# Seven block products instead of eight in the feed-forward up projection of a two-layer decoder

## The chip, the cores and the metric

The program runs on one core of a Trainium2 chip. The metric is the device time of one execution in microseconds (us); 2150.83 us is the median of three runs before the change (2150.53 to 2151.25). Engines are named as in the profile: PE is TensorE (PEld its weight loads), DVE is VectorE, ACT is ScalarE, POOL is GpSimd, SP is the SyncE queue, which issues all DMAs here. A matmul has a stationary operand of 128x128, which is loaded first, and streams a moving operand of up to 512 columns past it; its output goes to PSUM, which has eight banks of 128x512 float32.

## The reference

Two decoder layers on 512 tokens of 1024 channels. A layer mixes tokens in three branches and then runs a gated feed-forward block; only the latter changes:

```python
def conv_ffn(h, w_up, conv_w, conv_b, w_down):
    a, b = jnp.split(h @ w_up, 2, axis=-1)          # w_up: 1024 x (2 * 2816)
    ap = jnp.pad(a, ((0, 0), (CONV_WIDTH - 1, 0), (0, 0)))
    a = conv_b + sum(conv_w[j] * ap[:, j:j + s_len] for j in range(CONV_WIDTH))
    return (jax.nn.silu(a) * b) @ w_down            # w_down: 2816 x 1024

for l in range(2):
    ...
    x = x + merged @ w_out[l]
    x = x + conv_ffn(rms_norm(x, ffn_norm_g[l]), ...)
```

All values are float32.

## The kernel before

**Precision.** A float32 product runs as three matmuls of type float32r. An operand is split into hi (rounded to float32r) and lo (the rest), and hi*hi, hi*lo and lo*hi add up in PSUM (`mm3`, L173 to L179, one line for each of the three). So every weight has to be split on the core: `chunk` (L151) loads 512 KB of packed weights, a tile `raw` of 128x1024 (L155, on SP, three buffers), ACT casts it to `whi` (L158), DVE subtracts to get `wlo` (L159); whi and wlo have five buffers each.

**Norm.** `norm_tile` (L400) handles 128 tokens of x: squares and sums on ACT (L406), three small steps on POOL (L408 to L410), the scaling to `hn` on DVE (L413), and then `rest`: eight transposes on PE (L184), and for each half of the channels a cast to `hth` (ACT, L421) and a subtraction to `htl` (DVE, L422). hth and htl hold the normed x with channels on the partitions, 8 blocks of 128 channels by 512 tokens. With `wait=2`, `rest` is put off by two units of matmul work (`later`, `tick`, `due`), so that PE does not stand waiting for the norm. The output projection `add_out` with w_out (L966) does that after each token tile.

**Up projection and gate.** `ffn` (L981) takes the 2816 hidden features in 22 tiles of 128, in three passes of 8, 8 and 6. For a tile, `proj_t` (L443) computes the 128 features of a for all 512 tokens, 8 blocks of channels x 3 = 24 matmuls of 512 columns with the weights stationary, and later the same for b: 48 matmuls a tile, two weight chunks. The first tile is an exception: its a, its b and the a of the second tile are computed in two halves of 256 tokens (`halves=2`), with `flush` between them, which brings the put-off transposes of the last token tile. Then come the convolution (ACT L993, DVE L994 and L995), tanh for the silu (L1000), the gate (L1001, L1002), and the split of the result into `gh` (ACT, L1005) and a slice of brh or brl (DVE, L1006).

**Down projection.** At the end of a pass, `add_out` with w_down: for each half of the 1024 output channels and each of four token tiles 8 (or 6) features x 3 matmuls of 512 columns, with the gated tiles stationary and the weights moving, into a bank `acc` (three of them), and DVE adds it to x (L973). In the last pass of layer 0 the next layer's norm hangs on it, in the last pass of layer 1 the store of the output.

**Order.** The program is written as one sequence. A scheduler at build time orders the instructions of each engine by their place in it and by when their operands should be there, hands out tile buffers, and sets the semaphores. On the chip each engine runs its own list strictly in order.

Of the kernel before, what the change touches and what calls it, by code (L numbers as in the profile page):

```python
"""Two hybrid decoder layers (differential attention, dilated window attention, S5 SSM, gated
merge, convolutional gated MLP) on one core.

float32 matrix products run as three float32r products: an operand is split exactly into
hi (rounded to float32r) and lo (the rest), and hi*hi + hi*lo + lo*hi accumulate in PSUM.
"""
# [10 lines left out]
F32 = mybir.dt.float32  # L17
# [18 lines left out]
# S5 channels within a tile of 8 groups x 16 channels: partition = channel * 8 + group  # L36
UPERM = np.arange(512).reshape(4, 8, 16).transpose(0, 2, 1).reshape(512)

# columns of the small per-layer parameters
PK_BG, PK_GT, PK_SUB, PK_CW, PK_CB, PK_D, PK_BGLU, PK_N = 0, 24, 28, 29, 95, 117, 121, 125  # L40

BUFS = dict(raw=3, whi=5, wlo=5, qkv=20, acc=9, tmp=10, brh=1, brl=1, ct=1, gn=1)

# steps of side work per unit of a projection: SSM, attention
# [3 lines left out]
class Stream:  # L48
    """side work in steps: a step advances every running generator by one stage and starts the
    next one, so that the stages of successive generators are interleaved"""  # L50
# [26 lines left out]
class Alone:  # L77
    """a generator that starts when all before it have ended, and lets no other run beside it"""
# [5 lines left out]
class Net:  # L84
# [66 lines left out]
    def chunk(self, *spec):  # L151
        i = len(self.specs)
        self.specs.append(spec)
        raw = self.slot("raw", "raw", (128, 1024))
        self.nc.sync.dma_start(raw, self.io["wpk"][i])  # L155
        hi = self.slot("whi", "whi", (128, 1024), F32R)
        lo = self.slot("wlo", "wlo", (128, 1024), F32R)
        self.A.copy(hi, raw)  # L158
        self.V.tensor_tensor(lo, raw, hi.bitcast(F32), op=SUB)  # L159
        return hi, lo  # L160

    def slab(self, w, l, k0, nk, c0, before=None):
        """chunks for [nk*128, 512] of a weight; -> list over k of (hi, lo) [128, 512]"""
# [9 lines left out]
    def mm3(self, out, pairs):  # L173
        """out = sum over (stationary hi, lo), (moving hi, lo)"""
# [34 lines left out]
    def sincos(self, sin, cos, x, cols):  # L209
        """sin and cos of x [128, cols] (may overwrite x)"""  # L210
# [37 lines left out]
    def setup(self):  # L248
# [11 lines left out]
        # halves for sigmoids by tanh  # L260
# [3 lines left out]
        # columns for evacuating transposed q, k: gains times the score scale  # L264
# [5 lines left out]
        # angles: rope A (4 tiles x 8), rope B (2 orders x 4 tiles x 16), S5 (L x 16)  # L270
# [14 lines left out]
        # S5 scalars of both layers  # L285
# [18 lines left out]
        # f = (lambda - 1) / a  # L304
# [15 lines left out]
        # mag^8, and the unit phase exp(8 i theta)  # L320
# [12 lines left out]
    def layer_lambda(self, l):  # L333
        """lambda of the differential attention"""
# [17 lines left out]
    def layer_tables(self, l):  # L352
        """rope tables with gains and score scale; powers of the S5 lambda"""
# [17 lines left out]
        # powers of lambda, d = 0..8  # L371
# [8 lines left out]
    def cmul_step(self, tab, n, first, g):  # L380
        """tab[.., first+n : first+2n] = tab[.., first : first+n] * (element first+n-1 from `first`=1,
        or the n-th power kept apart): used for tables of powers that start at power 1"""
# [583 lines left out]
    def add_out(self, xt, w, l, k0, tiles, out=None, then=None):  # L966
        for s in range(2):
            ws = self.slab(w, l, k0, len(tiles), s * 512)
            for t in range(4):
# [6 lines left out]
                if s == 1 and then:  # L976
                    then(t)
# [233 lines left out]
```

## Time and profile before

| | us |
|---|---|
| median of three runs | 2150.83 |
| the profiled execution, first to last instruction | 2149.5 |
| PE busy | 2118.8 (99%) |
| DVE busy | 1163.7 (54%) |
| ACT busy | 869.8 (40%) |
| POOL busy | 149.3 (7%) |
| mean granted clock of TensorE | 1.000 |

The profiled execution's own time is its span, 2149.5 us; 1.3 us lie around it. Busy is the time in which at least one instruction of an engine ran. Matmuls are pipelined: the next one starts before the last has ended, so a matmul's duration (about 390 ns for 512 columns) is longer than the step from one start to the next, and the step is what it costs in a row. Layer 0's feed-forward block lies from about 711 to 1082 us, layer 1's from about 1777 to the end.

### The profile page before, as it was taken

The page shows a single profiled execution, that of the slowest core. Times are in us where ns is not written, and L with a number is a line of the kernel's source. Part 1 is how long each engine was busy: PE and PEld are TensorE (multiplying, and loading weights), DVE is VectorE, ACT ScalarE, POOL GpSimd, SP SyncE. Part 2 cuts the span into 40 slices and gives each one's busy share as a digit, 9 for nine tenths or more (in the row PEclk, how much of TensorE's full clock was granted, in tenths as well). Part 3 has the DMA queues.
Part 4 walks back from the last instruction along what each step waited for, and adds up shares of the span by engine and source line. Part 5 has one row for each costly group of instructions (what it writes and reads, how often), then busy time and mean ns, then how long its engine had stood idle before and what let it go on. Part 6 is the DMA issues. An engine that isn't in the chain of part 4 may idle for free.

```text
span 2149.5 us, 28401 instructions
## 1 busy us (share of the span) xinstructions
PE 2118.8 (99%) x10742; PEld 1787.5 (83%) x10742; DVE 1163.7 (54%) x2589; ACT 869.8 (40%) x1789; POOL 149.3 (7%) x299
## 2 busy tenths in 40 slices
PE   7999999999999999999999999999999999999999
PEld 5877899988888888888888778999888888888887
DVE  6757565556544653544447575554564446445353
ACT  4355555463232432323334546464532324223131
POOL 1211111100000000000002102010000000000000
PEclk9999999999999999999999999999999999999999
DMA  5331221533433323323342312224334323233231
GB/s 185 99 100 40 60 81 59 136 113 99 137 98 93 108 92 95 98 89 98 118 123 64 96 42 68 85 68 123 113 108 129 102 73 108 88 106 92 77 118 59
DMA packets 97257, 206.40 MB, mean 96 GB/s; under 512 B 40544, under 2 KB 45408, under 8 KB 97120
## 3 DMA queue, kind: packets, MB, share of 16 engines
q1 hardware_dynamic: 97120, 204.58, 30.8%
q8 instruction: 85, 1.39, 0.3%
q14 instruction: 52, 0.43, 0.1%
HBM read 193.01 MB, written 11.53 MB: 95 GB/s over the span
## 4 chain that ended last, share of the span: by engine, by line
PE 88%; DVE 5%; ACT 4%; POOL 1%; DMA 1%; issue 1%; SPq 0%; ACTq 0%; DVEq 0%; POOLq 0%
PE pacc L179 26%; PE pacc L177 26%; PE pacc L178 26%; PE ptp L184 2%; PE ps L542 1%; PE po L639 1%; PE ps L615 1%; ACT qn L483 1%; PE ps L863 1%; DMA raw<-wpk 1%; ACT sq L474 1%; DVE wlo L159 1%; POOL qr L477 1%; PE ps L860 1%; PE ps L698 1%
## 5 line engine op out<-in xcount | busy, mean ns | idle before, releaser
L158 ACT CAST whi<-raw 128x1024 fp32r<-128x1024 f32 x328 | 343.7, 1054 | 676.6 <-PE pacc L178 403.9
L159 DVE TENSOR_TENSOR wlo<-raw,whi 128x1024 fp32r<-128x1024 f32 x328 | 399.0, 1223 | 401.0 <-ACT whi L158 394.4
L179 PE MATMUL pacc<-hth,wlo 128*128 128x512 f32 (+1 forms) x1200 | 460.7, 384 | 0.0
L177 PE MATMUL pacc<-hth,whi 128*128 128x512 f32 (+1 forms) x1200 | 458.6, 383 | 0.5 <-ACT hth L421 0.5
L178 PE MATMUL pacc<-htl,whi 128*128 128x512 f32 (+1 forms) x1200 | 458.7, 382 | 0.2
L177 PE MATMUL pacc<-whi,hth 128*128 128x512 f32 x768 | 319.8, 418 | 0.0
L178 PE MATMUL pacc<-wlo,hth 128*128 128x512 f32 x768 | 308.4, 402 | 3.2 <-DVE wlo L159 3.2
L179 PE MATMUL pacc<-whi,htl 128*128 128x512 f32 x768 | 310.4, 404 | 0.0
L178 PEld LDWEIGHTS pacc<-htl,whi 128*128 128x128 f32 x1200 | 225.4, 188 | 46.6 <-DVE htl L422 0.6
L177 PEld LDWEIGHTS pacc<-hth,whi 128*128 128x128 f32 x1200 | 225.1, 188 | 45.0 <-ACT hth L421 1.0
L179 PEld LDWEIGHTS pacc<-hth,wlo 128*128 128x128 f32 x1200 | 225.5, 188 | 43.8
L178 PEld LDWEIGHTS pacc<-wlo,hth 128*128 128x128 f32 x768 | 192.3, 251 | 18.9 <-DVE wlo L159 4.1
L179 PEld LDWEIGHTS pacc<-whi,htl 128*128 128x128 f32 x768 | 191.4, 249 | 16.5
L177 PEld LDWEIGHTS pacc<-whi,hth 128*128 128x128 f32 x768 | 191.3, 249 | 15.6 <-ACT hth L421 0.2
L177 PE MATMUL pacc<-whi,gh 128*128 128x512 f32 x352 | 139.9, 397 | 0.0
L178 PE MATMUL pacc<-wlo,gh 128*128 128x512 f32 x352 | 139.3, 396 | 0.0
L973 DVE TENSOR_TENSOR x<-x,pacc 128x512 f32<-128x512 f32 x64 | 44.0, 687 | 158.9 <-PE pacc L179 158.9
L178 PEld LDWEIGHTS pacc<-wlo,gh 128*128 128x128 f32 x352 | 66.1, 188 | 16.5
L177 PEld LDWEIGHTS pacc<-whi,gh 128*128 128x128 f32 x352 | 66.2, 188 | 16.0
L179 PE MATMUL pacc<-whi,brh 128*128 128x512 f32 x192 | 76.3, 397 | 0.0
L477 POOL TENSOR_TENSOR qr<-qr,mhalf 128x4 f32<-128x4 f32 (+1 forms) x64 | 75.6, 1181 | 5.3
L474 ACT ACTIVATE sq<-pacc 128x128 f32<-128x128 f32 x192 | 50.6, 284 | 41.1 <-PE pacc L179 40.9
(302 smaller groups left out, 2871.0 us busy)
## 6 DMA issues: line engine op xcount, KB each, us to landing
raw<-wpk SPq DMA_DIRECT2D x328, 512.0 KB, 3.7
x<-x SPq DMA_DIRECT2D x16, 256.0 KB, 6.0
gn<-ng SPq DMA_DIRECT2D x4, 512.0 KB, 5.8
u_d<-uS SPq DMA_DIRECT2D x8, 256.0 KB, 2.8
u<-u_d SPq DMA_DIRECT2D x8, 256.0 KB, 4.9
y_d<-ys SPq DMA_DIRECT2D x8, 256.0 KB, 2.2
ym<-y_d SPq DMA_DIRECT2D x8, 256.0 KB, 4.6
um<-u_d SPq DMA_DIRECT2D x8, 256.0 KB, 4.0
```

What stands on the lines that cost most here:

```text
L158: self.A.copy(hi, raw)
L159: self.V.tensor_tensor(lo, raw, hi.bitcast(F32), op=SUB)
L177: self.PE.matmul(out, lhsT=ah, rhs=bh, start=i == 0, stop=False)
L178: self.PE.matmul(out, lhsT=ah, rhs=bl, start=False, stop=False)
L179: self.PE.matmul(out, lhsT=al, rhs=bh, start=False, stop=i == n - 1)
L184: self.PE.transpose(tp[:, b * 128 : b * 128 + 128], src[:, b * 128 : b * 128 + 128], self.ident)
L474: A.activation(sq[:, h * dh : h * dh + dh], av[:, h], AF.Square, accum_out=ss[:, h : h + 1])
L477: G.tensor_tensor(r, r, self.mhalf[:, :heads], op=ALU.pow)
L483: A.activation(qv[:, h], qv[:, h], AF.Copy, scale=r[:, h : h + 1])
L542: PE.matmul(reg, lhsT=q[64 * j : 64 * j + 64, h * 128 : h * 128 + 128], rhs=k[kt][64 * j : 64 * j + 64, h * 128 : h * 128 + 128], start=kt ...
L615: PE.matmul(s[:, c : c + 128], lhsT=q[:, h * 128 : h * 128 + 128], rhs=k[kb][:, h * 128 : h * 128 + 128], start=h == h0 and b == 0, stop=F ...
L973: self.V.tensor_tensor(xt[t][s], xt[t][s], acc, op=ADD)
```

## The change

With the channels of the input in two halves (0 to 511, 512 to 1023) and the tokens in two halves (0 to 255, 256 to 511), the up projection of a quad of feature tiles (two of a, two of b) is a product of 2 x 2 blocks: eight block products of 512 channels, 256 features and 256 tokens. The new kernel forms it from seven (the Strassen scheme in Winograd's form).

- **Input blocks.** `fnorm_tile` takes the place of `norm_tile` ahead of the feed-forward block. Tokens 0 to 255 (tiles 0 and 1) give the operands 11 and 12 (the two channel halves) and are kept unsplit as well; once tokens 256 to 511 (tiles 2 and 3) are there, it forms s3 = x11 - x21, s1 = x22 - x21, s2 = -s1 - x11, s4 = -s2 - x12 and 22, and splits each into hi and lo. `flush` runs before the block, so the put-off part of the last tile now comes before its first product in the program.
- **Weight blocks.** A quad loads four blocks of 512 channels x 256 features (as many chunks as before), forms four sums of them on DVE (`wsum`), and splits seven operands: 7 casts on ACT and 7 subtractions on DVE, where four chunks had 4 of each.
- **Products.** `xprod` runs one block product: 2 feature tiles x 4 channel blocks x 3 = 24 matmuls of 256 columns into one bank, the first feature tile in columns 0 to 255 of the bank, the second in columns 256 to 511.
- **Partial sums.** Sums that are used twice stay in PSUM. ACT copies bank x0 to y0 after the first product, and y0 to y1 after the third, and later products add to what lies there; one matmul of the identity into y0 and y1 at the start of the block readies the banks for that. The product s3 is copied out to s7 and added by DVE.
- **Gate.** Convolution, tanh, gate and split now work on the two feature tiles of a quad together, tanh and one gate step on 128x1024.
- **Down projection.** Six passes of 2, 4, 4, 4, 4, 4 feature tiles instead of 8, 8, 6; `add_half` does one half of the output channels of a pass behind each quad of the next pass, the last pass's two halves at the end.
- **Buffers.** Six raw buffers instead of three, one of them taken by the weight sums of a quad; `gh` in the tag acc; a new tag y4. `dynamic_dma_scratch_size` is set to 128. Comments are taken out throughout.

The diff, without the hunks that only drop comments:

```diff
-BUFS = dict(raw=3, whi=5, wlo=5, qkv=20, acc=9, tmp=10, brh=1, brl=1, ct=1, gn=1)
+BUFS = dict(raw=6, whi=5, wlo=5, qkv=20, acc=9, tmp=10, brh=1, brl=1, ct=1, gn=1, y4=1)
+SCRATCH = 128
...
+    def load(self, *spec):
         i = len(self.specs)
         self.specs.append(spec)
         raw = self.slot("raw", "raw", (128, 1024))
         self.nc.sync.dma_start(raw, self.io["wpk"][i])
+        return raw
+    def wsplit(self, raw):
         hi = self.slot("whi", "whi", (128, 1024), F32R)
         lo = self.slot("wlo", "wlo", (128, 1024), F32R)
         self.A.copy(hi, raw)
         self.V.tensor_tensor(lo, raw, hi.bitcast(F32), op=SUB)
         return hi, lo
 
+    def chunk(self, *spec):
+        return self.wsplit(self.load(*spec))
...
-    def norm_tile(self, xt, t, wait=0):
+    def norm_rows(self, xt, t):
...
+        return hs
+    def norm_tile(self, xt, t, wait=0):
+        V, A = self.V, self.A
+        hs = self.norm_rows(xt, t)
...
+    def fnorm_begin(self, which):
+        self.norm_begin(which)
+        ops = {n: [] for n in ("11", "12", "22", "s1", "s2", "s3", "s4")}
+        for x in (self.hth, self.htl):
+            flat = x.rearrange("p k q -> p (k q)").rearrange("p (b k q) -> p b k q", b=4, k=4)
+            for i, n in enumerate(("22", "s1", "s2", "s3")):
+                ops[n].append([flat[:, i]])
+        for n in ("11", "12", "s4"):
+            for x in "hl":
+                ops[n].append([self.slot("qkv", "x" + n + x, (128, 2, 256), F32R) for _ in range(2)])
+        self.xop = ops
+        self.x1 = self.slot("y4", "x11", (128, 4, 256)), self.slot("ct", "x12", (128, 4, 256))
+    def xsplit(self, n, src, c):
+        hi, lo = self.xop[n]
+        w = 4 // len(hi)
+        for i, (h, l) in enumerate(zip(hi, lo)):
+            s = src[:, i * w : i * w + w]
+            self.A.copy(h[:, :, c], s)
+            self.V.tensor_tensor(l[:, :, c], s, h[:, :, c].bitcast(F32), op=SUB)
+    def fnorm_tile(self, xt, t, wait=0):
+        V, A = self.V, self.A
+        hs = self.norm_rows(xt, t)
+        x11, x12 = self.x1
+        v4 = lambda a: a.rearrange("p (k q) -> p k q", k=4)
+        def rest():
+            c = slice((t % 2) * 128, (t % 2) * 128 + 128)
+            tp = [v4(self.transpose4(hs[h])) for h in range(2)]
+            if t < 2:
+                for n, x, dst in zip(("11", "12"), tp, self.x1):
+                    self.xsplit(n, x, c)
+                    A.copy(dst[:, :, c], x)
+                return
+            x21, s3, s1, s2, s4 = (v4(self.slot("tmp", "xs")) for _ in range(5))
+            A.copy(x21, tp[0])
+            V.tensor_tensor(s3, x11[:, :, c], x21, op=SUB)
+            self.xsplit("s3", s3, c)
+            V.tensor_tensor(s1, tp[1], x21, op=SUB)
+            V.scalar_tensor_tensor(s2, s1, -1.0, x11[:, :, c], op0=MUL, op1=SUB)
+            self.xsplit("s2", s2, c)
+            self.xsplit("s1", s1, c)
+            self.xsplit("22", tp[1], c)
+            V.scalar_tensor_tensor(s4, s2, -1.0, x12[:, :, c], op0=MUL, op1=SUB)
+            self.xsplit("s4", s4, c)
...
-    def add_out(self, xt, w, l, k0, tiles, out=None, then=None):
+    def add_out(self, xt, w, l, k0, tiles, then):
         for s in range(2):
             ws = self.slab(w, l, k0, len(tiles), s * 512)
             for t in range(4):
@@ -971,45 +1039,117 @@
                 tk = slice(t * 128, t * 128 + 128)
                 self.mm3(acc, [((tiles[k][0][:, tk], tiles[k][1][:, tk]), ws[k]) for k in range(len(tiles))])
                 self.V.tensor_tensor(xt[t][s], xt[t][s], acc, op=ADD)
-                if out is not None:
-                    self.nc.sync.dma_start(out[tk, s * 512 : s * 512 + 512], xt[t][s])
-                if s == 1 and then:
+                if s == 1:
...
+    def xprod(self, bank, w, n, start):
+        wh, wl = (x.rearrange("p (k f) -> p k f", k=4) for x in w)
+        hi, lo = self.xop[n]
+        per = 4 // len(hi)
+        mm = self.PE.matmul
+        for s in range(2):
+            o = bank[:, s * 256 : s * 256 + 256]
+            fs = slice(s * 128, s * 128 + 128)
+            for k in range(4):
+                xh, xl = hi[k // per][:, k % per], lo[k // per][:, k % per]
+                mm(o, lhsT=wh[:, k, fs], rhs=xh, start=start and s == k == 0, stop=False, skip_group_check=True)
+                mm(o, lhsT=wh[:, k, fs], rhs=xl, start=False, stop=False, skip_group_check=True)
+                mm(o, lhsT=wl[:, k, fs], rhs=xh, start=False, stop=k == 3, skip_group_check=True)
+    def wsum(self, out, a, b):
+        self.V.tensor_tensor(out, a, b, op=ADD)
+        return out
+    def ffn_quad(self, l, f, y0, y1, lo_out):
+        V, A = self.V, self.A
+        ca, cb = f * 128, DFF + f * 128
+        w11 = self.load("s", "w_up", l, 0, ca)
+        w12 = self.load("s", "w_up", l, 0, cb)
+        w22 = self.load("s", "w_up", l, 512, cb)
+        tw = self.slot("raw", "tw", (128, 1024))
+        w21 = self.load("s", "w_up", l, 512, ca)
+        x0 = self.psum("o")
+        self.xprod(x0, self.wsplit(w11), "11", True)
+        A.copy(y0, x0)
+        x1 = self.psum("tp")
+        self.xprod(x1, self.wsplit(self.wsum(tw, w12, w22)), "s3", True)
+        s7 = self.slot("tmp", "s7")
+        A.copy(s7, x1)
+        self.xprod(y0, self.wsplit(self.wsum(tw, tw, w11)), "s2", False)
+        A.copy(y1, y0)
+        self.xprod(x0, self.wsplit(w21), "12", False)
+        a = self.slot("ct", "ua", (128, 2, 512))
+        half = lambda v: v.rearrange("p (s q) -> p s q", s=2)
+        A.copy(a[:, :, :256], half(x0))
+        self.xprod(y1, self.wsplit(self.wsum(w12, w12, w11)), "s1", False)
+        b2 = self.slot("tmp", "ub2")
+        V.tensor_tensor(b2, y1, s7, op=ADD)
+        self.xprod(y0, self.wsplit(self.wsum(tw, tw, w21)), "22", False)
+        V.tensor_tensor(a[:, :, 256:], half(y0), half(s7), op=ADD)
+        self.tick()
+        self.xprod(y1, self.wsplit(w22), "s4", False)
+        b1 = self.slot("tmp", "ub1")
+        A.copy(b1, y1)
+        y = self.slot("y4", "uy", (128, 2, 512))
+        for s in range(2):
+            cw = lambda j: self.pk[:, l, PK_CW + 3 * (f + s) + j : PK_CW + 3 * (f + s) + j + 1]
+            A.activation(y[:, s], a[:, s], AF.Identity, scale=cw(2), bias=self.pk[:, l, PK_CB + f + s : PK_CB + f + s + 1])
+            V.scalar_tensor_tensor(y[:, s, 1:], a[:, s, :511], cw(1), y[:, s, 1:], op0=MUL, op1=ADD)
+            V.scalar_tensor_tensor(y[:, s, 2:], a[:, s, :510], cw(0), y[:, s, 2:], op0=MUL, op1=ADD)
+        A.activation(a, y, AF.Tanh, scale=0.5)
+        V.scalar_tensor_tensor(y, a, 1.0, y, op0=ADD, op1=MUL)
+        for h, b in enumerate((b1, b2)):
+            yh = y[:, :, h * 256 : h * 256 + 256]
+            V.tensor_tensor(yh, yh, half(b), op=MUL)
+        gated = []
+        for s in range(2):
+            hi, lo = self.slot("acc", "gh", dt=F32R), lo_out[:, s]
+            A.activation(hi, y[:, s], AF.Copy, scale=-0.5)
+            V.scalar_tensor_tensor(lo, y[:, s], -0.5, hi.bitcast(F32), op0=MUL, op1=SUB)
+            gated.append((hi, lo))
+        self.tick()
+        return gated
     def ffn(self, l, xt, out, then):
-        V, A = self.V, self.A
-        for p, (f0, nf) in enumerate(((0, 8), (8, 8), (16, 6))):
...
-            self.add_out(xt, "w_down", l, f0, gated, out if end else None, then if end else None)
+        los = self.branch_tiles()
+        y0, y1 = self.psum("s"), self.psum("s")
+        for y in (y0, y1):
+            self.PE.matmul(y, lhsT=self.identr, rhs=self.identr.unsqueeze(1).broadcast_to([128, 4, 128]), start=True, stop=True)
+        before = None
+        f = 0
+        for p, quads in enumerate((1, 2, 2, 2, 2, 2)):
+            f0, gated = f, []
+            for i in range(quads):
+                gated += self.ffn_quad(l, f, y0, y1, los[p % 2][:, 2 * i : 2 * i + 2])
+                if before:
+                    self.add_half(xt, l, i, *before)
+                f += 2
+            before = f0, gated
+        for s in range(2):
+            self.add_half(xt, l, s, *before, out, then)
+    def add_half(self, xt, l, s, k0, tiles, out=None, then=None):
+        ws = self.slab("w_down", l, k0, len(tiles), s * 512)
+        for t in range(4):
+            acc = self.psum("acc")
+            tk = slice(t * 128, t * 128 + 128)
+            self.mm3(acc, [((tiles[k][0][:, tk], tiles[k][1][:, tk]), ws[k]) for k in range(len(tiles))])
+            self.V.tensor_tensor(xt[t][s], xt[t][s], acc, op=ADD)
+            if out is not None:
+                self.nc.sync.dma_start(out[tk, s * 512 : s * 512 + 512], xt[t][s])
+            if s == 1 and then:
+                then(t)
+            self.tick()
...
-            self.norm_begin(2 * l + 1)
-            self.add_out(xt, "w_out", l, 0, self.mg, then=lambda t: self.norm_tile(xt, t, 2))
+            self.fnorm_begin(2 * l + 1)
+            self.add_out(xt, "w_out", l, 0, self.mg, then=lambda t: self.fnorm_tile(xt, t, 2))
+            self.flush()
...
+        elif sp[0] == "s":
+            r, c = sp[3], sp[4]
+            out[i] = w[r : r + 512, c : c + 256].reshape(4, 128, 256).transpose(1, 0, 2).reshape(128, 1024)
...
-    nc = bacc.Bacc("TRN2", target_bir_lowering=False, num_devices=1)
+    nc = bacc.Bacc("TRN2", target_bir_lowering=False, num_devices=1, dynamic_dma_scratch_size=SCRATCH)
```

## Rows read from the trace of the kernel before

**Rows 1.** Busy time, share of the span and instructions of each engine, whole program.

```profile
PE 2118.8 (99%) x10742; PEld 1787.5 (83%) x10742; DVE 1163.7 (54%) x2589; ACT 869.8 (40%) x1789; POOL 149.3 (7%) x299
```

**Rows 2.** Stretches of layer 0: up, then down projection; busy us, instructions, clock, DMA.

```profile
735.00:801.00 66.00, 66.00 (x290) 54.13 (x290) 35.12 (x43) 24.36 (x31) 0.00 (x0) 1.00 0.31 97
...
801.00:848.00 47.00, 47.00 (x201) 37.52 (x200) 16.11 (x18) 9.01 (x10) 0.00 (x0) 1.00 0.22 70
```

**Rows 3.** What PE waited for, whole program: us in total, times, longest.

```profile
PE ptp L184 <- DVE hn L413: 13.2, 3, 12.5
...
PE pacc L178 <- DVE wlo L159: 3.2, 2, 1.6
```

**Rows 4.** Timeline of PE, first feature tiles: start us, duration us, engine, line, operation.

```profile
712.41 0.28 PE L178 MATMUL pacc<-htl,whi 128*128 128x256 f32 x1
...
720.34 0.28 PE L179 MATMUL pacc<-hth,wlo 128*128 128x256 f32 x1
...
722.69 0.28 PE L179 MATMUL pacc<-hth,wlo 128*128 128x256 f32 x1
...
730.58 0.28 PE L179 MATMUL pacc<-hth,wlo 128*128 128x256 f32 x1
...
735.04 0.39 PE L178 MATMUL pacc<-htl,whi 128*128 128x512 f32 x1
...
750.15 0.39 PE L178 MATMUL pacc<-htl,whi 128*128 128x512 f32 x1
```

**Rows 5.** Timeline of DVE: instructions in a row, start and total duration.

```profile
709.94 3.49 DVE L159 TENSOR_TENSOR wlo<-raw,whi 128x1024 fp32r<-128x1024 f32 x3
...
713.94 1.28 DVE L422 TENSOR_TENSOR htl<-ptp,hth 128x512 fp32r<-128x512 f32 x2
```

**Rows 6.** Groups of DVE by shape: busy us, mean ns, idle before them and its releaser.

```profile
L159 DVE TENSOR_TENSOR wlo<-raw,whi 128x1024 fp32r<-128x1024 f32 x328 | 399.0, 1223 | 401.0 <-ACT whi L158 394.4 <-PE po L639 5.4
...
L995 DVE SCALAR_TENSOR_TENSOR cv<-pacc,pk,cv 128x510 f32<-128x510 f32 x44 | 32.9, 749 | 1.5
```

**Rows 7.** Groups of ACT by shape, same columns.

```profile
L158 ACT CAST whi<-raw 128x1024 fp32r<-128x1024 f32 x328 | 343.7, 1054 | 676.6 <-PE pacc L178 403.9 <-PE pacc L179 193.0 <-DMA raw<-wpk 49.5
...
L993 ACT ACTIVATE cv<-pacc,pk 128x512 f32<-128x512 f32 x44 | 34.1, 774 | 0.0
...
L1000 ACT ACTIVATE fth<-cv 128x512 f32<-128x512 f32 x44 | 27.9, 633 | 89.2 <-DVE cv L995 89.1
...
L1005 ACT ACTIVATE gh<-cv 128x512 fp32r<-128x512 f32 x44 | 27.7, 630 | 0.4 <-DVE cv L1002 0.4
...
L507 ACT COPY v<-pacc 128x512 f32<-128x512 f32 x32 | 18.8, 588 | 56.4 <-PE pacc L179 56.2
```

**Rows 8.** Timeline of PE, DVE and POOL at the last token tile's norm, layer 0.

```profile
711.18 0.40 PE L179 MATMUL pacc<-whi,ml 128*128 128x512 f32 x1
...
713.35 0.68 DVE L973 TENSOR_TENSOR x<-x,pacc 128x512 f32<-128x512 f32 x1
...
715.42 0.55 POOL L410 TENSOR_TENSOR nr<-nr,mhalf 128x1 f32<-128x1 f32 x1
...
716.00 1.42 DVE L413 SCALAR_TENSOR_TENSOR hn<-x,nr,gn 128x512 f32<-128x512 f32 x2 [0.78 <-POOL nr L410]
...
720.46 1.03 PE L184 MATMUL ptp<-identr,hn 128*128 128x128 f32 x8
...
721.74 0.62 PE L177 MATMUL pacc<-hth,whi 128*128 128x256 f32 x3 [0.24 <-ACT hth L421]
```

**Rows 9.** Timeline of DVE within the gate of a feature tile, layer 0.

```profile
736.70 0.69 DVE L1002 TENSOR_TENSOR cv<-cv,pacc 128x512 f32<-128x512 f32 x1
...
737.30 1.22 DVE L159 TENSOR_TENSOR wlo<-raw,whi 128x1024 fp32r<-128x1024 f32 x1
...
738.43 0.69 DVE L1006 SCALAR_TENSOR_TENSOR brh<-cv,gh 128x512 fp32r<-128x512 f32 x1
```

**Rows 10.** A group of weight loads (PEld): busy us, mean ns, idle before.

```profile
L178 PEld LDWEIGHTS pacc<-htl,whi 128*128 128x128 f32 x1200 | 225.4, 188 | 46.6 <-DVE htl L422 0.6
```

More of the change, by code (lines that the diff above doesn't have):

```diff
@@ L148, in psum @@
         return self.ps.tile(list(shape), F32, tag=tag, bufs=b, name=self.nm(f"p{tag}"))
-    def chunk(self, *spec):
+    def load(self, *spec):
         i = len(self.specs)
@@ L422, in rest @@
                 V.tensor_tensor(lo, tp, hi.bitcast(F32), op=SUB)
+        if wait:
+            self.later(wait, rest)
+        else:
+            rest()
+    def fnorm_begin(self, which):
[41 more added lines that the diff above has]
+            self.xsplit("s4", s4, c)
         if wait:
@@ L973, in add_out @@
                 self.V.tensor_tensor(xt[t][s], xt[t][s], acc, op=ADD)
-                if out is not None:
-                    self.nc.sync.dma_start(out[tk, s * 512 : s * 512 + 512], xt[t][s])
-                if s == 1 and then:
+                if s == 1:
                     then(t)
                 self.tick()
-    def ffn(self, l, xt, out, then):
-        V, A = self.V, self.A
-        for p, (f0, nf) in enumerate(((0, 8), (8, 8), (16, 6))):
-            gated = []
-            los = self.branch_tiles()
-            for f in range(f0, f0 + nf):
-                if f == 0:
-                    pa, pb, pa1 = self.proj_t("w_up", l, 0, DFF, 128, halves=2)
-                else:
-                    pa = pa1 if f == 1 else self.proj_t("w_up", l, f * 128)
-                y = self.slot("tmp", "cv")
-                cw = lambda j: self.pk[:, l, PK_CW + 3 * f + j : PK_CW + 3 * f + j + 1]
-                A.activation(y, pa, AF.Identity, scale=cw(2), bias=self.pk[:, l, PK_CB + f : PK_CB + f + 1])
-                V.scalar_tensor_tensor(y[:, 1:], pa[:, :511], cw(1), y[:, 1:], op0=MUL, op1=ADD)
-                V.scalar_tensor_tensor(y[:, 2:], pa[:, :510], cw(0), y[:, 2:], op0=MUL, op1=ADD)
-                self.tick()
-                if f > 0:
-                    pb = self.proj_t("w_up", l, DFF + f * 128)
-                th = self.slot("tmp", "fth")
-                A.activation(th, y, AF.Tanh, scale=0.5)
-                V.scalar_tensor_tensor(y, th, 1.0, y, op0=ADD, op1=MUL)
-                V.tensor_tensor(y, y, pb, op=MUL)
-                hi = self.slot("acc" if p == 1 else "qkv", "gh", dt=F32R)
-                lo = los[(f - f0) // 4][:, (f - f0) % 4]
-                A.activation(hi, y, AF.Copy, scale=0.5)
-                V.scalar_tensor_tensor(lo, y, 0.5, hi.bitcast(F32), op0=MUL, op1=SUB)
-                gated.append((hi, lo))
-                self.tick()
-            end = f0 + nf == NF
-            self.add_out(xt, "w_down", l, f0, gated, out if end else None, then if end else None)
```

## The prediction

> **What bounds the kernel now.** I read the busy shares first: PE is busy for 2118.8 of 2149.5 us, every other engine for at most 54% of it [rows 1]. The stretch table says the same of the feed-forward part: 66 us of the up projection have 66.00 us of PE, 35.12 of DVE and 24.36 of ACT, the down projection 47 of 47, and the granted clock is 1.00 throughout [rows 2]. The list of what PE waited for has 13.2 us for the first norm, 3.2 for weight splits in the whole program, little else [rows 3]. So only fewer or cheaper matmuls shorten this program, and work put on DVE and ACT costs nothing until one of them is late. A busy PE says nothing of its pace, so the price of a matmul is taken from start to start, in the timeline. From 735.04 to 750.15 there are 66 steps of 512 columns, 228.9 ns each. The first feature tile already runs in halves of 256 columns: 70 steps from 712.41 to 720.34, 113.3 ns each (tokens 0 to 255), and 67 from 722.69 to 730.58, 117.8 ns each (the other half) [rows 4]. Half the columns cost half the time, each with its own weight load.
>
> **The change, part by part.** The sum is made against the profiled span of 2149.5 us; the median of the runs is 2150.8, so 1.3 is added at the end.
>
> *Products.* Before, a layer has 41 chunks of 24 matmuls at 0.2289 and three of 48 at the mean of 0.1133 and 0.1178: 225.2 + 16.6 = 241.9 us. After, each of 11 quads has 7 x 24 = 168 matmuls of 256 columns. I take the mean, 0.1155: 19.4 us a quad, 213.5 a layer, because half of the outputs lie in the upper half of their bank as those of the second stretch did; the ends are 19.0 and 19.8 us a quad. Two identity matmuls of 512 columns add 0.5. Gain 27.9 a layer, **55.9 in both** (47 to 65). The Trainium skill, "TensorE: Matmul & The Clock Gate", section on the back-to-back issue gap, speaks against this: it gives 81 ns for sustained pairs of load and matmul at 128 columns and 131 at 512, so a straight line puts 256 columns at an estimated 98, 168 of them at 16.4 and 96 of 512 at 12.6, and the kernel would lose some 84 us. This trace has 228.9 at 512 [rows 4], so I hold that rule for wrong here.
>
> *Down projection.* The same 528 matmuls a layer; six passes instead of three, so 48 additions into x instead of 24, on DVE beside PE. Its matmuls run at 47 us for 200, 235 ns [rows 2].
>
> *What VectorE gets.* A 128x1024 subtraction takes 1223 ns in the mean [rows 6], but three in a row take 3.49 us, so the third starts 2.26 after the first: 1.13 each. Two of 512 columns in a row: 1.28, thus about 0.60 each [rows 5]. A full quad with its half of the down projection (four feature tiles) asks for: nine split subtractions and four sums of weight blocks (priced as the split, the only 128x1024 row) and one 1024-wide gate, 14 x 1.13 = 15.8; four convolution steps at 0.75 [rows 6], 3.0; ten of 512 columns, 6.0. Together 24.8 us, against PE's 19.4 + 48 x 0.235 = 30.7: 81%. With a half of two feature tiles it is 23.7 against 25.0: 95%. ACT: nine casts at 1.05, five copies out of or into PSUM at 0.6 (the PSUM to PSUM copy has no row; the nearest is 588 ns), two at 0.77, tanh as two of 0.63, two roundings at 0.63 [rows 7]: 16.5 us, 54%. So ACT is cover enough and **VectorE is the engine to watch**.
>
> *The seeds.* The copy y0 from x0 has the second product to hide in, y1 from y0 the fourth, b2 the sixth: 2.8 us each, for 0.6 and the wait behind a cast of 1.05 [rows 7]. Cost 0; without that cover 0.6 to 1.7 each, three a quad.
>
> *The seam before the up projection.* Before, tokens 0 to 255 of three chunks (72 matmuls, 712.2 to 720.5) stood between the last w_out matmul at 711.18 and the transposes of token tile 3; x was added at 713.35, POOL ended near 716.0, the norm ran to 717.4, and PE lost 0.24 us [rows 8]. Now only the first product (2.8 us) needs no second half. Before the seventh product can begin, VectorE owes: addition 0.6, norm 1.4, the five new operands of tiles 2 and 3 (four combinations, four subtractions at 0.60, two short ones at 0.35: 5.5 each, 11.0), six splits and three sums 10.2, b2 0.6: 23.8 us. PE's own work up to there is 1.7 of transposes, 0.5, six products 16.6: 18.8. That is 5.0 us lost a layer if VectorE never waits. It does wait, for POOL (0.78) [rows 8] and for the chain transpose, copy, difference, cast, subtraction; I add 3. **8 a layer** (5 to 18). A stop this long could drop the clock, 1.00 in all stretches here; at the lower level one product would take 2.8 more, which lies inside that range.
>
> *Quads two and three* run at 95%, starting without a lead: 2 a layer (0 to 10). *Eight full quads* at 81%: the lead is five weight buffers, VectorE executes in order, and each subtraction needs its cast first. The order of before puts a split between two gate steps (737.30 and 738.43) [rows 9], so gaps are filled: 0.5 each, 4 a layer (0 to 20). *The last quad* has 4 x 12 x 0.235 = 11.3 us of the previous pass to hide its gating, about 10 us in series, beside 4.7 us of splits and additions: 1 a layer (0 to 3).
>
> *Loads.* SP issues the same 328 chunks. A quad holds five of six raw buffers, but its blocks come free as their sums are formed, well before the next quad's splits. A weight split kept PE waiting 3.2 us [rows 3]; three more buffers could give that back elsewhere, or push another load behind: 0 (plus or minus 3). Next layer's norm: units shrink from 18 to 12 matmuls, so two units, 5.6 us, stand against 4.1 us from addition to norm [rows 8]: 0 (to 1.5).
>
> **Sum:** 2149.5 - 55.9 + 2 x (8 + 2 + 4 + 1) = 2123.6, with 1.3 about **2125 us**.
>
> **The rivals.**
> *VectorE becomes the bound (slower).* Before, the splits waited 394.4 us for their casts, 1.2 each [rows 6]. That is free at 54%, not at 81%. If the four chains sum, cast, subtraction of a quad each leave 1.05 idle and the gating leaves 3.4 (two convolution starts, tanh, rounding), a full quad takes 24.8 + 4.2 + 3.4 = 32.4 instead of 30.7, a quad with a short half 31.3 instead of 25.0, the seam 14 (5.0, six casts, 3 of the chain), the end 3: 14 + 2 x 6.3 + 8 x 1.7 + 3 = 43 a layer, 86 in all: 2181. It decides from 28 us a layer, 2.5 a quad. For it: strict order on one engine. Against it stand the filled gaps [rows 9].
> *Everything is hidden but the floor of the seam:* 2150.8 - 55.9 + 10 = 2105. For it: ACT at 54% and five buffers; against: the 95% of two quads.
> *The product saved is no time saved:* in steady state a 256-column matmul is paced by its weight load. A load lasts 188 ns [rows 10]; were it not overlapped, a quad would take 168 x 0.188 = 31.6, 9.6 more than before, and the program 2363. It breaks even at 131 ns a matmul. But 70 in a row came at 113 [rows 4]. The rule of the Trainium skill above would lie in this corner too, with its estimated 2235.
>
> **How the numbers follow.** The forecast, 2112 to 2140, gets 0.53; the hidden case 0.2; VectorE as the bound, 2145 to 2195, 0.23; the weight load 0.04. A measurement of this kernel can tell about 0.2%, 4.3 us, from no change. Of the third case I put 0.05 below 2146.5, 0.06 within, 0.12 above. Faster 0.78, same 0.06, slower 0.16. The range runs from 2100, under the hidden case with a price between 0.1133 and 0.1155, to 2155, into the VectorE case; about 2 in 10 lie outside.
>
> **What the next profile would show.** Right: some 3700 matmuls of 256 columns at 113 to 118 ns, PE busy about 60 us less, a gap of 6 to 10 us before the second product of each layer, DVE near 80% between. Wrong: a gap of over 2.5 us in every quad with a split's subtraction as releaser (VectorE), waits of PE for the seed copies (the cover failed), or steps near 130 ns without gaps (the price). Hardly any gap even at the seam would mean 2105.

## Result and profile after

The changed kernel takes **2118.33 us** in the median of four runs (2114.02 to 2125.94), against 2150.77 for the kernel before beside it: a ratio of 0.985 (95% interval 0.983 to 0.987), 1.5% less time. The profiled execution took 2119.21 us, its span is 2117.4, the mean granted clock 0.996.

The busy line of the page, for [rows 1]:

```profile
PE 2073.6 (98%) x12186; PEld 1821.6 (86%) x12186; DVE 1397.9 (66%) x2853; ACT 1002.3 (47%) x1979; POOL 149.8 (7%) x299
```

PE is busy 45.2 us less, and its share falls from 99% to 98%: there are gaps now. The stretch table of layer 0 says where, for [rows 2] (columns: stretch, its length, then busy us and instructions of PE, PEld, DVE, ACT and POOL, the granted clock, DMA share, GB/s):

```profile
711.00:738.00 27.00, 19.73 (x138) 18.22 (x137) 22.69 (x32) 16.28 (x28) 1.35 (x3) 0.87 0.25 82
738.00:800.00 62.00, 62.00 (x482) 59.81 (x481) 60.27 (x71) 35.35 (x46) 0.00 (x0) 1.00 0.28 93
800.00:900.00 100.00, 99.68 (x705) 92.90 (x705) 82.72 (x91) 51.89 (x64) 0.00 (x0) 1.00 0.37 121
900.00:1000.00 100.00, 100.00 (x711) 93.42 (x710) 82.03 (x91) 50.87 (x62) 0.00 (x0) 1.00 0.30 101
```

Most of what PE loses in these four stretches lies in the first 27 us. This is the seam: the stretch from the last output projection to the end of the first quad, in which the input operands are formed. Behind it VectorE is at 97% for 62 us and PE does not miss a nanosecond, then VectorE settles at 82% and ACT at 51%. What PE waited for, for [rows 3]:

```profile
PE ptp L191 <- DVE hn L420: 15.4, 6, 11.8
PE ptp L1058 <- ACT hth L463: 3.5, 2, 1.7
PE pacc L185 <- DVE wlo L163: 3.2, 2, 1.6
PE ptp L191 <- DVE htl L464: 2.4, 2, 2.0
PE ps L1058 <- ACT ps L1084: 2.4, 2, 1.4
...
PE po L1060 <- DVE wlo L163: 1.7, 2, 0.8
PE ptp L1059 <- DVE htl L464: 1.5, 2, 0.8
PE ps L1058 <- DVE ub L1091: 1.2, 2, 0.9
```

Most new entries come twice, once a layer. The 3.2 us of the weight split stayed as they were, so six raw buffers gave nothing back there. Now the seam on PE, for [rows 8], the steps with a wait and some behind them (timeline, layer 0):

```profile
716.36 0.63 PE L191 MATMUL ptp<-identr,hn 128*128 128x128 f32 x4 [0.70 <-DVE hn L420]
...
718.06 0.39 PE L1060 MATMUL po<-x12h,wlo 128*128 128x256 f32 x1 [0.83 <-DVE wlo L163]
...
722.89 0.63 PE L191 MATMUL ptp<-identr,hn 128*128 128x128 f32 x4 [1.98 <-DVE htl L464]
725.27 0.58 PE L1058 MATMUL ptp<-hth,whi 128*128 128x256 f32 x1 [1.75 <-ACT hth L463]
726.48 0.58 PE L1059 MATMUL ptp<-htl,whi 128*128 128x256 f32 x1 [0.63 <-DVE htl L464]
726.86 0.41 PE L1060 MATMUL ptp<-hth,wlo 128*128 128x256 f32 x1
727.08 0.41 PE L1058 MATMUL ptp<-hth,whi 128*128 128x256 f32 x1
...
730.68 0.28 PE L1060 MATMUL ptp<-hth,wlo 128*128 128x256 f32 x1
730.80 0.28 PE L1058 MATMUL ptp<-hth,whi 128*128 128x256 f32 x1
...
735.52 0.38 PE L1058 MATMUL ps<-hth,whi 128*128 128x256 f32 x1 [1.38 <-ACT ps L1084]
```

These are six waits, 7.3 us in all. PE runs block 12 (`x12h`) as the second product, ahead of s3, although the program has it fourth. From 726.86 to 730.68 there are seventeen steps of 213 instead of 118 ns and one of 195. The stretch table shows the clock there:

```profile
723.00:725.00 2.00, 0.52 (x4) 0.28 (x4) 2.00 (x5) 1.01 (x3) 0.00 (x0) 0.70 0.09 31
725.00:731.00 6.00, 5.10 (x23) 4.81 (x24) 5.57 (x9) 1.94 (x4) 0.00 (x0) 0.53 0.00 0
```

Cut finer, the granted clock is 1.00 from 720.6 to 723.8, where PE was busy for 0.95 us, and 0.50 from 723.8 to 730.6, the lower level, 1.2 GHz. In layer 1 it is 0.50 twice, from 1771.7 to 1775.1 and from 1778.5 to 1785.3, with 42 slow steps, 4.0 us, against the 1.7 us of layer 0; the waits are shorter there, 5.5 us. VectorE in the same microseconds of layer 0, and two rows of ACT:

```profile
717.92 0.69 DVE L482 TENSOR_TENSOR xs<-x,xs 128x512 f32<-128x512 f32 x1
718.52 0.69 DVE L484 TENSOR_TENSOR xs<-ptp,xs 128x512 f32<-128x512 f32 x1
719.12 1.22 DVE L163 TENSOR_TENSOR wlo<-raw,whi 128x1024 fp32r<-128x1024 f32 x1
720.26 0.69 DVE L464 TENSOR_TENSOR htl<-xs,hth 128x512 fp32r<-128x512 f32 x1
720.86 0.69 DVE L485 SCALAR_TENSOR_TENSOR xs<-xs,x 128x512 f32<-128x512 f32 x1
721.46 0.69 DVE L464 TENSOR_TENSOR htl<-xs,hth 128x512 fp32r<-128x512 f32 x1
722.06 0.69 DVE L464 TENSOR_TENSOR htl<-ptp,hth 128x512 fp32r<-128x512 f32 x1
...
723.86 0.69 DVE L482 TENSOR_TENSOR xs<-x,xs 128x512 f32<-128x512 f32 x1
...
725.73 0.69 DVE L464 TENSOR_TENSOR htl<-xs,hth 128x512 fp32r<-128x512 f32 x1
...
722.11 0.58 ACT L481 COPY xs<-ptp 128x512 f32<-128x512 f32 x1
...
724.60 0.61 ACT L463 CAST hth<-xs 128x512 fp32r<-128x512 f32 x1
```

VectorE forms what it can of tile 2 before tile 3's s3 (line 482, 717.92 and again 723.86), though the next product on PE needs s3 of both tiles alone. The second four transposes of tile 3 (722.89) also wait until the bank `ptp` of tile 2 has been read for the last time, by the subtraction of block 22 at 722.06. By these rows that wait cost nothing by itself: s3 of tile 3 needs the first four transposes (716.36) alone. ACT copied those out at 722.11, VectorE formed the difference at 723.86, and its cast ended at 725.21, just before PE went on at 725.27.

**Ledger of a layer** (each start-to-start step beyond its usual length counted as loss):

| us | layer 0 | layer 1 |
|---|---|---|
| feed-forward block before, after | 369.9, 357.8 | 368.2, 349.2 |
| lost in the seam before, after | 0.96, 10.85 | 0.96, 11.32 |
| lost elsewhere before, after | 0.16, 2.63 | 0, 1.56 |

The blocks give 12.1 and 19.0 us, the rest of the program 0.9: together the 32.1 us between the two spans. Nearly all of the 7 us that layer 1 gains more has one cause: 1438 of its 1848 steps of 256 columns take 113.3 ns, while nearly all of layer 0 take 117.8; 4.5 ns on 1438 steps are 6.5 us.

### The profile page after: what moved, and what is told of

Read it like the earlier page. It is cut to its first block, busy times and chain, and to the rows that moved or that the text cites. A ratio compares the mean times of both kernels' runs of the same rounds, so it can differ in the third digit from the quotient of the medians.

```text
span 2117.4 us, 31698 instructions
## 1 busy us (share of the span) xinstructions
PE 2073.6 (98%) x12186; PEld 1821.6 (86%) x12186; DVE 1397.9 (66%) x2853; ACT 1002.3 (47%) x1979; POOL 149.8 (7%) x299
## 4 chain that ended last, share of the span: by engine, by line
PE 85%; DVE 7%; ACT 4%; POOL 2%; issue 1%; DMA 1%; SPq 0%; POOLq 0%; ACTq 0%; DVEq 0%
PE pacc L184 19%; PE pacc L186 19%; PE pacc L185 19%; PE ps L1060 3%; PE ps L1058 3%; PE ps L1059 3%; PE ptp L191 2%; PE po L1060 2%; PE po L1059 2%; PE po L1058 2%; DVE wlo L163 1%; PE ps L610 1%; PE po L707 1%; PE ptp L1059 1%; PE ptp L1060 1%
## 5 line engine op out<-in xcount | busy, mean ns | idle before, releaser
L184 PE MATMUL pacc<-hth,whi 128*128 128x512 f32 x448 | 176.3, 394 | 0.0
L186 PE MATMUL pacc<-hth,wlo 128*128 128x512 f32 x448 | 175.9, 393 | 0.0
L185 PE MATMUL pacc<-htl,whi 128*128 128x512 f32 x448 | 175.4, 392 | 0.0
L1058 PE MATMUL ps<-hth,whi 128*128 128x256 f32 x528 | 147.2, 279 | 2.4 <-ACT ps L1084 2.4
L1060 PE MATMUL ps<-hth,wlo 128*128 128x256 f32 x528 | 147.2, 279 | 0.1
L1059 PE MATMUL ps<-htl,whi 128*128 128x256 f32 x528 | 146.9, 278 | 0.0
L186 PEld LDWEIGHTS pacc<-hth,wlo 128*128 128x128 f32 x448 | 84.2, 188 | 18.0
L185 PEld LDWEIGHTS pacc<-htl,whi 128*128 128x128 f32 x448 | 84.1, 188 | 18.0
L1060 PEld LDWEIGHTS ps<-hth,wlo 128*128 128x128 f32 x528 | 99.3, 188 | 0.3 <-DVE wlo L163 0.3
L1059 PEld LDWEIGHTS ps<-htl,whi 128*128 128x128 f32 x528 | 99.5, 188 | 0.0
```

The costliest lines, as they stand in the source:

```text
L184: self.PE.matmul(out, lhsT=ah, rhs=bh, start=i == 0, stop=False)
L185: self.PE.matmul(out, lhsT=ah, rhs=bl, start=False, stop=False)
L186: self.PE.matmul(out, lhsT=al, rhs=bh, start=False, stop=i == n - 1)
L1058: mm(o, lhsT=wh[:, k, fs], rhs=xh, start=start and s == k == 0, stop=False, skip_group_check=True)
L1059: mm(o, lhsT=wh[:, k, fs], rhs=xl, start=False, stop=False, skip_group_check=True)
L1060: mm(o, lhsT=wl[:, k, fs], rhs=xh, start=False, stop=k == 3, skip_group_check=True)
```

## The experiments

**The changed kernel again**, unchanged, beside the first group, and later beside the last.

> The changed kernel once more, nothing edited. Theory (the pace of a 256-column matmul, 113 or 118 ns, is not tied to a place in the program but is set anew by a wait of PE and kept until the next): the quads that ran at 118 (all of layer 0, the first of layer 1) and at 113 (the last seven of layer 1) change places in part, each quad that changes moves the span by 168 x 4.5 ns = 0.76 us, and the span differs from 2117.4 us by several us; the two seams before the up projection still lose 10 to 13 us each. Rival (the pace belongs to the addresses of a quad): the same quads at the same pace, span within 1 us of 2117.4.

Measured: 2124.22 us (2117.64 to 2126.99), ratio 0.987 (0.986 to 0.989). Here layer 1 ran at 117.8 ns too and took 354.7 us instead of 349.2, with the same losses in the seam (10.73 and 11.32).

> The changed kernel once more, as it is, beside the two versions with it in this call. Its median lies between 2118 and 2127 by all theories, near the lower end if the 256-column products of a layer run at 113 ns a step and near the upper if all run at 118 ns.

Measured: 2122.97 us (2120.69 to 2125.34), ratio 0.987 (0.986 to 0.988); layer 1 had 1205 of its 1848 steps at 113 ns and took 348.9 us. Over the twelve runs of this kernel the median is 2122.7. Its range of 13 us, where the kernel before stays within 4, fits this pace, since a whole layer at 113 instead of 118 ns makes up to 8 us (1848 x 4.5 ns); a difference of 2 or 3 us has to be read from the seam in the trace, not from the time.

**Eight products in the new structure**: sums, differences and seeds gone, everything else kept.

```diff
-        self.xprod(x0, self.wsplit(w11), "11", True)
-        A.copy(y0, x0)
...
+        w = self.wsplit(w11)
+        self.xprod(x0, w, "11", True)
+        self.xprod(y0, w, "s3", True)
+        w = self.wsplit(w21)
+        self.xprod(x0, w, "12", False)
+        self.xprod(y0, w, "22", False)
```

> Eight block products instead of seven in the otherwise changed kernel: no sums of weights, no seeds, four splits a quad, and tiles 2 and 3 give only 21 and 22. Theory (the gain is the columns saved, VectorE bounds nothing but the seam): 24 x 117.8 ns = 2.8 us more for each of 22 quads, 62 us, less most of the two seams, 16 to 20 us: about 2165, slower than the kernel before by 10 to 18 us, since 256-column matmuls at 118 ns cost more than half of one of 512. Rival (VectorE holds PE up throughout): relieved of its sums and splits, it loses less than half of that, under 2140.

Measured: 2167.45 us. Two stretches of layer 0, columns as above:

```profile
711.00:738.00 27.00, 25.86 (x213) 25.20 (x212) 16.64 (x21) 12.85 (x19) 0.93 (x3) 1.00 0.46 152
...
800.00:900.00 100.00, 100.00 (x711) 93.42 (x710) 49.27 (x57) 36.22 (x45) 0.00 (x0) 1.00 0.28 90
```

Every quad of 192 steps takes 22.61 us, one of 168 in the changed kernel at the same pace 19.79: the difference is the 24 steps, 2.82 us. The seam costs 1.8 us in both layers, so about 9 of the 11 us belong to the new operands of input and weights, not to the new norm or to the halves. The block takes 9.2 and 7.4 us more than before though it loses hardly anything: a quad's eight products at 117.8 ns cost 22.61 us, four chunks of 512 columns 4 x 24 x 0.2289 = 21.97.

**Seeds left out.** The sums that the two copies start with are then missing from the result.

```diff
-        A.copy(y0, x0)
...
-        A.copy(y1, y0)
```

> The two copies of ACT from bank to bank (y0 from x0, y1 from y0) are left out, so the partial sums are not seeded and two of the four blocks are not those of the reference. Theory (the seeds lie under the next product): the ten full quads of a layer already have no gap, so only the waits named for the copies go, 2.4 us in all, and the time is 0 to 5 us below 2118. Rival (the seeds hold PE up a little in each quad): 0.6 us or more for each of 44 copies, 26 us or more off.

Measured: 2127.85 us, not below the changed kernel beside it (2124.22). The 2.4 us of "ps <- ACT ps" are gone from the list of waits, and 1.8 us for weight splits stand there that were not there, 1.5 more for the transposes. So leaving them out gains nothing: in full quads no wait shows with or without them, and in the first the next wait is right behind. That the first quad waits for the copy y1 at all (1.38 us in layer 0, 1.0 in layer 1) comes of the order on PE: block 12, which was to cover that copy, had been run second, so product s1 follows s2 directly. In the other quads block 12 stands between them, and there is no such wait.

**Both halves of the down projection behind their own pass.**

```diff
-                if before:
-                    self.add_half(xt, l, i, *before)
                 f += 2
-            before = f0, gated
+            for s in range(2):
+                self.add_half(xt, l, s, f0, gated, *end)
```

> Both halves of a pass's down projection follow directly behind its own quads, as before the change, instead of between the quads of the next pass. Theory (the interleaving is what hides the gating of a quad, some 10 us in series): PE gets gaps of 3 to 8 us at most of the 12 pass ends, 36 to 96 us in all, more than the change gains. Rival (the order that the scheduler finds hides it anyway, as it did before): less than 10 us slower than 2118.

Measured: 2140.98 us, 16.8 above the changed kernel beside it, between the two theories. Its list of waits has one large new entry:

```profile
PE pacc L184 <- ACT gh L1112: 12.9, 10, 2.3
```

The gating now ends after PE has come to the matmuls that need it: ten of the twelve passes end with a wait for it, 0.6 to 2.3 us. Interleaving is worth 9 to 11 us a layer here (11.4 and 11.6 us lost outside the seam, against 2.4 and 0.6); the rest of the gating in series hides behind the next products, which need nothing from it.

**Another order of the token tiles** in w_out, so that the rows needed later come in earlier.

```diff
-            for t in range(4):
+            for t in (0, 2, 1, 3) if s == 1 else range(4):
```

> The second half of the w_out projection takes its token tiles in the order 0, 2, 1, 3, so that the five operands of tile 2 (5.5 us of VectorE) are formed while PE still works on tiles 1 and 3. Theory (VectorE's queue sets the seam): the loss of a seam falls from about 11 us by 4 to 5 us, 8 to 10 us in all, about 2109. Rival (the chain of the last tile's norm, POOL and transposes sets it): the last tile's chain is as long as before and the time stays within 2 us of the changed kernel.

Measured: 2127.84 us (2120.54 to 2129.44), ratio 0.988 (0.986 to 0.990), no gain. The wait moved:

```profile
PE ptp L191 <- DVE hn L420: 14.8, 4, 12.7
PE po L1059 <- DVE x11l L464: 9.3, 4, 2.9
```

Now the first product waits for tile 1, and the seam loses 12.6 and 12.7. The granted clock is at 0.50 for 10.3 us of it in layer 0, longer than before. So moving a tile ahead moves the wait to another tile. That the whole work between the norm and the products is the limit fits this, but is not shown by it.

**Some subtractions on POOL.**

```diff
-            self.V.tensor_tensor(l[:, :, c], s, h[:, :, c].bitcast(F32), op=SUB)
+            (self.G if n in ("s1", "s2", "s4") else self.V).tensor_tensor(l[:, :, c], s, h[:, :, c].bitcast(F32), op=SUB)
```

> The subtractions that form the lo parts of s1, s2 and s4 (4 of 128x512 and 4 of 128x256 a layer for tiles 2 and 3) go to POOL, order unchanged. Theory (order on VectorE, s3 first in line): VectorE has 3.8 us less to do before s3 of tile 3 is formed, so the loss of a seam falls by 2 to 4 us, if POOL takes no more than about 2 us for one. Rival (POOL is far slower than VectorE at this): PE waits for POOL instead and the loss grows.

Measured: 2128.87 us; the seam loses 12.5 a layer. The groups of POOL (busy us, mean ns of one, idle before):

```profile
L464 POOL TENSOR_TENSOR htl<-xs,hth 128x512 fp32r<-128x512 f32 x8 | 15.5, 1949 | 11.6 <-ACT hth L463 11.6
L464 POOL TENSOR_TENSOR xs4l<-xs,xs4h 128x256 fp32r<-128x256 f32 x8 | 12.6, 1593 | 0.0
```

A subtraction that VectorE does in 0.60 us of a row takes POOL 1.95.

**Operands product by product**: s3 of both tiles first, then s2 of both, and so on; block x22 is copied out by ACT at once, which also sets the bank free for the transposes of tile 3.

```diff
+            A.copy(x22, tp[1])
+            self.second.append((c, x21, x22))
+            if t < 3:
+                return
+            for c, x21, x22 in self.second:
...
+                self.xsplit("s2", s2, c)
...
+            for c, x22, s1, s2 in seconds:
+                self.xsplit("s1", s1, c)
```

> In the seam the operands of tiles 2 and 3 are formed product by product instead of tile by tile: s3 of both tiles first, then s2 of both, then s1, 22 and s4; x22 is copied out of PSUM by ACT for that. Theory (PE waits for the product s3 because VectorE, strictly in order, forms all five operands of tile 2 before the first of tile 3): s3 starts about 5 us earlier, of the 10.8 us that a seam loses (as steps above their usual length) 3 to 5 go, 6 to 10 us in all, about 2113 at the slow pace of 118 ns against 2122 for the same kernel unedited. Rival (the sum of VectorE's work up to the seventh product sets the seam, whatever its order): the waits move to later products and the loss stays within 1.5 us of 10.8.

Measured: 2118.10 us (2114.66 to 2123.79), ratio 0.985 (0.983 to 0.987). The seam loses 7.44 and 7.49 instead of 10.85 and 11.32, and the granted clock stays at 1.00 in it. Once more, beside the changed kernel:

> The operands formed product by product once more, as they were. Theory A (VectorE's order in the first quad is what the seam loses): 7.4 us of waits and slow steps a layer there instead of 11 us, so 6 to 8 us under the unchanged version where both run at the same pace. Rival B (the earlier gain was the pace of the steps): no more than 2 us apart, both with ranges of about 10 us.

Measured: 2119.73 us (2119.07 to 2120.61) against 2122.97, ratio 0.986 (0.984 to 0.987). Nearly all steps of this profile are at 118 ns, so theory A holds for the seam (7.26 and 7.40). But 3.2 us between the medians is half of what was expected, and the 2113 us expected of the first run at that pace were missed too. Its list of waits shows what was given back:

```profile
PE ps L1071 <- ACT ps L1097: 2.4, 2, 1.2
...
PE ps L1073 <- DVE wlo L163: 1.5, 2, 0.8
```

The third quad, which lost nothing, now loses 1.56 us a layer to weight casts and splits that come late (whi, wlo): PE leaves the seam earlier, VectorE does not, since from 717 to 740 it is busy for 22.9 of 23 us, and its 97% stretch begins, as I read it, without a lead. The two intervals overlap; the gain over the changed kernel is what the trace shows, not what the times alone prove.

What the seam no longer loses is, as the rows count it, for the larger part the lower clock. PE's waits in it are 5.3 us instead of 7.2 in layer 0, and 5.5 in both versions in layer 1; the rest of the gain is steps of 213 ns that no longer come. That the new order keeps the clock up because PE no longer stands idle so long at one place is argued: no run told order and clock apart.

**Block 22 and s4 later still.**

```diff
         A.copy(a[:, :, :256], half(x0))
+        if f == 0:
+            self.last("22")
...
+        if f == 0:
+            self.last("s4")
         b2 = self.slot("tmp", "ub2")
```

> As product by product, and also block 22's splits and the whole of s4 move behind the first quad's weight operands, in every engine's program. Theory A (the ScalarE copy y1<-y0 starts late because the casts of s4 stand ahead of it and wait for VectorE): the 1.3 us wait for that copy goes, about 1 us a layer, 2 us in all. Rival: s4's own operands are then late at the last product of the first quad, a wait of 1 to 2 us there, no gain or 2 us slower.

Measured: 2119.51 us (2112.98 to 2120.99), ratio 0.985 (0.983 to 0.986): no different from the version before it. Theory A falls; the wait for the copy is as long as it was (1.3 us). ACT's timeline, layer 0:

```profile
731.70 1.05 ACT L162 CAST whi<-tw 128x1024 fp32r<-128x1024 f32 x1 [0.26 <-DVE tw L1079]
732.65 0.58 ACT L1100 COPY ps<-ps 128x512 f32<-128x512 f32 x1
```

What stands ahead of the copy is a weight cast that waits for a weight sum, VectorE again. The rival's late s4 did not come either.

**The kernel before with the new buffers.**

```diff
-BUFS = dict(raw=3, whi=5,
+BUFS = dict(raw=6, whi=5,
...
-    nc = bacc.Bacc("TRN2", target_bir_lowering=False, num_devices=1)
+    nc = bacc.Bacc("TRN2", target_bir_lowering=False, num_devices=1, dynamic_dma_scratch_size=128)
```

> The kernel before with six raw buffers instead of three and the dynamic_dma_scratch_size of the changed one, nothing else. Theory (the loads were already early enough): within 3 us of the kernel before. Rival (deeper loads shorten the other stages, and are part of the gain): 5 us or more faster.

Measured: 2150.40 us against 2150.66, ratio 1.000 (0.999 to 1.001). The buffers bring nothing by themselves.

## Why the prediction was right, and where its sizes were off

The direction, the main term and the place of the main loss held; 2125 was forecast for 2118.33 (2122.7 over all twelve runs). That the sum came so close is in part luck: the seam was forecast too small and the full quads too large, and the two partly cancel. Step by step:

- **Products: 55.9 forecast, 53.9 measured.** Layer 0's 1848 steps at 117.8 ns leave 23.7 of 241.9 us, layer 1's mix (1438 at 113.3) 30.2. The mean of the two prices was right by its size and wrong by its reason: the pace has nothing to do with where in the bank the output lies, since whole quads run at one or the other. The kernel with eight products shows the term alone. On the rule of the Trainium skill ("TensorE: Matmul & The Clock Gate", back-to-back issue gap) the trace decides: no stretch of 256 columns here went below 113 ns, where its figures gave an estimated 98.
- **VectorE: 81% forecast, 82% measured; 95% and 97%; ACT 54% and 51%.** The two unseen prices were right (groups of the page):

```profile
L1063 DVE TENSOR_TENSOR tw<-tw,raw 128x1024 f32<-128x1024 f32 x44 | 53.7, 1221 | 0.0
...
L1084 ACT COPY ps<-ps 128x512 f32<-128x512 f32 x22 | 12.8, 581 | 0.0
```

- **The seam: 8 a layer forecast, 9.9 and 10.4 more than before measured.** This term was too small, though inside its 5 to 18. The floor of 5.0 counted VectorE's work up to the seventh product as if it came in the order in which PE needs it; "I add 3" for waits and the chain was to cover the rest. It came tile by tile instead, and PE stood longest before s3, the first product that needs tile 3. "Only the first product needs no second half" was wrong: block 12 needs none either and ran second, so the stop does not lie before the second product, as the signs had it, but in six waits over the first five. Left out altogether was the bank that tile 2 holds until its block 22 is split (1.98 us at that wait, which by the rows above cost nothing by itself). The clock did drop, which was left inside the range: 1.7 us of slow steps in layer 0, 4.0 in layer 1. With the order mended and the bank set free (changed together, and the clock stayed up, so the three shares were not told apart) the seam loses 7.4, nearly the sum that was forecast.
- **Quads with little cover.** Quads two and three: 2 forecast; 0.6 and 1.5 measured in the two layers, most of it a quad later, in the first of the full quads. Seven full quads behind that: nothing measured, where 4 was forecast for all eight. At 82% VectorE is late for none of these. This was the largest single error, nearly 8 us over both layers, in the opposite direction to the seam.
- **Last quad and next norm: 1 and 0 forecast.** The last quad's gating cost nothing: no wait names it. The next layer's norm cost 1.7 us in layer 0 and 0.95 more right behind the block (in "the rest of the program"), beyond the 1.5 allowed. "Two units, 5.6 us" was misread: the norm is put on the list before the unit that it belongs to is counted off, so that only one unit of 12 matmuls, 2.8 us (1057.12 to 1059.92), lies before the transposes. PE waits for the norm there (its timeline, layer 0):

```profile
1061.03 0.66 PE L191 MATMUL ptp<-identr,hn 128*128 128x128 f32 x4 [0.72 <-DVE hn L420]
```

  The eight-product version, with VectorE at half load, has the same waits.
- **Seeds and loads at 0**: shown, by the versions without seeds and with the buffers alone. One of the prediction's own signs of being wrong, a wait of PE for a seed copy, does show, once a layer, where block 12 had left its place.
- **PE busy about 60 us less**: 45.2 measured. Of the 24 us lost only 13 are idle time of PE; the rest are slow steps and the first steps behind a wait, which count as busy.

The losses come to 12.4 and 11.9 us a layer instead of 15, the products to 2.0 us less, the rest of the program 0.9 better: 2123.6 - 5.7 + 2.0 - 0.9 = 2119.0 against a span of 2117.4. Of the 1.6 us left, 1.3 are the down projection, whose steps took 234.6 ns in the mean before and 233.3 after (1056 of them).

Of the rivals, VectorE as the bound (2181) failed at its premise: idle moments between cast and subtraction do not add up, other work fills them, even at 97%. The weight load as pace (2363) is refuted by 1848 steps at 118 ns. The case with all hidden but the floor (2105) was right for the full quads and wrong for the seam. The down projection's place, costed at nothing, is worth 17 us in all: that step of the change carries much of what the change brings (one run, 2140.98 beside 2124.22).

## What to carry to other kernels

Where a kernel is bound by matmuls at full pace, a product saved is time saved, steady stretches at 82% of the helping engine included; look for the loss at the seams, where several new operands must be there before PE may go on. There, emit the preparation in the order in which the consumer needs it, across tiles. And before believing 3 us, compare the same stretch in both traces: mending a seam can hand the delay to the stretch behind it, as here, 7.5 us won and 2.8 given back.

## What the runs showed of the hardware that was not expected

Matmuls of 256 columns run at one of two paces, 113.3 or 117.8 ns a step, at the same granted clock of 1.00, and keep it over hundreds of microseconds, through stretches of other shapes. A switch in the profiled execution (PE, layer 1):

```profile
1864.26 0.28 PE L1059 MATMUL ps<-htl,whi 128*128 128x256 f32 x1
1864.38 0.28 PE L1060 MATMUL ps<-hth,wlo 128*128 128x256 f32 x1
1865.54 0.38 PE L1058 MATMUL ps<-xs4h,whi 128*128 128x256 f32 x1 [0.88 <-DVE ub L1091]
...
1868.03 0.28 PE L1058 MATMUL ps<-xs4h,whi 128*128 128x256 f32 x1
1868.14 0.28 PE L1059 MATMUL ps<-xs4l,whi 128*128 128x256 f32 x1
1868.25 0.28 PE L1060 MATMUL ps<-xs4h,wlo 128*128 128x256 f32 x1
```

Steps of about 118 up to 1864.38, then a wait, then 113 to the end of the program: quads of 19.04 instead of 19.79 us. Over the ten profiled executions with seven products the pace changed mostly where PE had waited. Counting as a wait a step of at least 40 ns over its usual length, with six steps or more of 256 columns on either side: of 96 waits that began at 118, 13 ended at 113; of 13 that began at 113, 12 ended at 118; of 164 passages through other shapes without a wait, 163 kept it. Once it changed with neither: in the version with another order of the token tiles, a row without a gap goes from 118 to 113 at 757.6 and stays there for 7.6 us. So a program with few waits mostly keeps the pace that it has, but a wait is not the only occasion for a change. Why there are two was not found, and no run here could choose one.
